# Four of eight output weights converted during attention B, two output tiles contracted in halves, denominators inverted as compact rows

## The chip, the cores and the metric

The kernel runs on one core of a Trainium2 chip. The metric is the device time of one execution in microseconds (us); the figure that is compared is the median over timed executions. TensorE multiplies matrices (PE in the profile, PEld its weight loads), VectorE (DVE), ScalarE (ACT) and GpSimd (POOL) work on tiles, SyncE (SP) issues most of the DMAs. Each engine runs its own instruction list in order, and waits on semaphores where it needs another engine or a DMA.

## The reference, cut to what matters

Two layers of a decoder run on 1024 prompt tokens and 32 sample tokens (T = 1056), model width 1024. Layer 0 is a mixture of attention A (sliding window, with sinks) and attention B (three dilated groups whose outputs are merged by their softmax denominators), times a SiLU gate, followed by one output projection, residual and layer norm:

```
mix = concat([oa, ob], -1)                 # 512 + 512 columns
mix = mix * silu(z)
y   = mix @ w_out                          # 1024 x 1024
x1  = layer_norm(alpha * x + y)
```

Layer 1 is an mLSTM in chunks of 128 tokens with its own projections, output projection and layer norm. Besides y, the caches and the states are outputs.

## The kernel before, in words

All matrix products that need float32 accuracy are made of three products of split numbers: a high part (`hi`, ScalarE) and the rest (`lo`, usually VectorE), high times high, low times high and high times low. Tokens come in three chunks `CH` of 384, 384 and 288; a chunk holds three token tiles of 128, the last one two and the 32 samples.

Layer 0 goes in stages: projections and attention A, then the gate projections with the maxima of B, then attention B proper (`attn_b`, from about 485 to 642 us), then the output projection (`out0`, `out_proj`, from 642 us). `attn_b(kv)` takes the groups 3, 2, 1 in turn. For each block of 128 queries `scores` makes scores `sc` on PE, their exponentials twice on ScalarE (`ph` rounded, `p` exact), the difference `pl` = p - ph (line 477 on GpSimd for every fourth block, `POOL_LO`; line 114 on VectorE for the others), and three products into `av`: values by ph (lines 481, 482) and by pl (line 483). `emit` adds `av` into `OD`, [65, 4, 1024], whose last row is the denominators. Beside it runs `samples()`, the attention of the sample tokens, in scratch tiles `scr` with its keys and values loaded as `KT`.

`merge0(ty, kv, c, M)` makes two of the eight feature blocks of one chunk of `mix`: it loads `mo` (numerators) and `mf` (denominators, each row broadcast to 64 partitions), multiplies, multiplies by the gate `mz`, and splits into `mh` and `ml`. For kv = 0, `finish` has already inverted the denominators as a [32, 128] tile `dn` (line 511) and written them to `FD`. For kv = 1 (`inverse=False`), `mf` is loaded from the raw denominators in `OD` and inverted after the broadcast, on VectorE, 128 partitions by 384 columns, twice per chunk (line 839).

`out_proj` contracts `mix` with the eight weight blocks k = 0 to 7 of `w_out`. A weight block is loaded as `wr` (two buffers), and split into `oh` (ScalarE) and `ol` (VectorE). Blocks 0 and 1 are made during attention B; blocks 2 to 7 go into pool `wo`, which takes memory that attention B used. One token tile takes two PSUM tiles `py` (halves of the 1024 columns) with 24 products each, in k order: line 163 (mh by oh), 164 (ml by oh), 165 (mh by ol). Line 880 then adds the residual, and `layer_norm` and the transposes `trx` follow.

The order on each engine is not that of the source: the tile framework schedules the program by its own estimates of time, with priorities set by `ahead`, and `weave` mixes the streams by the weights W1 to W4. So a change in one place can move others.

Of the kernel before, what the change touches and what calls it, by code (L numbers as in the profile page):

```python
# [4 lines left out]
F32 = mybir.dt.float32  # L5
# [61 lines left out]
POOL_LO = 4  # L67

# [5 lines left out]
class Scratch:  # L74


    def __init__(self, *tiles):
        self.free = [[t, 0] for t in tiles]
        self.tags = {}

# [15 lines left out]
class Builder:  # L96
# [57 lines left out]
    def proj_tok(self, ps, i, X, xs, w):  # L154
# [3 lines left out]
        for k in range(8):  # L158
# [289 lines left out]
    def scores(self, g, kv, hf, Q1, Q2, K1, K2, V, emit):  # L448
        nc = self.nc
        for qb in range(2 * hf, 2 * hf + 2):  # L450
# [4 lines left out]
            for bi, (kb, kind) in enumerate(bl):  # L455
# [45 lines left out]
    def finish(self, ty, kv, sink_nm=None):  # L501
# [10 lines left out]
        self.store('m', self.FD[ty][kv].rearrange("h (b q) -> (h b) q", q=128), dn)  # L512

# [48 lines left out]
    def attn_b(self, kv, done=None):  # L562
# [253 lines left out]
    def merge0(self, ty, kv, c, M, inverse=True):  # L816
# [10 lines left out]
        OD = self.OD[ty][kv]  # L827
        D = self.FD[ty][kv] if inverse else OD[64]
        for u in range(2 * ty):
            pr = slice(64 * u, 64 * u + 64)  # L830
            self.load(o[pr, :, :m], OD[0:64].rearrange("d (c u) t -> d c u t", u=2)[:, :, u, t0:t0 + m])
            self.load(F[pr, :, :m], D.rearrange("(c u) t -> c u t", u=2)[:, u, t0:t0 + m].partition_broadcast(64))
# [29 lines left out]
    def out_proj(self, M, W, xres, g, b, consume, early={}):  # L862
        nc = self.nc
        with self.tc.tile_pool(name="lnp", bufs=3) as lp:
            for i in ORDER:
                m = 128 if i < 8 else 32
                if i == 6:
                    xs = self.pair(lp, M[2])
                xr = None
                if i in early:  # L870
                    r = early[i]
                else:
                    xr = lp.tile([128, 1024], F32, tag="xr", name="xr")
                    r = [xr[:, 0:512], xr[:, 512:1024]]
                    self.load(xr[:m], xres[128 * i:128 * i + m])
                for n in range(2):
                    ps = self.pp.tile([128, 512], F32, tag=("pj", "sc")[n], name="py")
                    ns = slice(512 * n, 512 * n + 512)
                    self.proj_tok(ps, i, M, xs if i == 8 else None, lambda k: [w[:, ns] for w in W[k]])
                    nc.vector.scalar_tensor_tensor(r[n][:m], r[n][:m], ALPHA, ps[:m], op0=OP.mult, op1=OP.add)  # L880
                    for c in (32,) if i == 8 else ():
                        nc.vector.tensor_tensor(r[n][:32], ps[c:c + 32], r[n][:32], OP.add)
                self.layer_norm(m, r, g, b)
                consume(i, m, r, xr)

    def layer0(self):
# [13 lines left out]
        self.FD = [[dt(f"FD{t}{i}", [4, TP]) for i in range(2)] for t in range(2)]  # L900
        self.SZ = dt("SZ", [8, 128, T])
# [9 lines left out]
        with tc.tile_pool(name="qp", bufs=2) as self.qp, tc.tile_pool(name="kp", bufs=2) as self.kp, \  # L911
# [81 lines left out]
            def samples():  # L993
                sp = Scratch(*(self.x2p.tile([128, 3072], F32, tag=f"x{u}x2", name=f"scr{u}") for u in "hl"))
# [643 lines left out]
```

## Time and profile before

| what | value |
|---|---|
| time, median of 3 runs | 1497.02 us (1495.68 to 1500.87) |
| the profiled execution: time, span | 1504.22 us, 1501.9 us |
| granted TensorE clock, mean | 0.979 of full |
| PE busy | 1416.9 us, 94% of the span |
| DVE, ACT, POOL busy | 896.6, 514.3, 203.1 us |

The span runs from the first to the last instruction; the rest of an execution's time lies around it. The page has the busy time of each engine in 40 slices; of PE's 40 digits the lowest, a 7, is the slice from 638 to 676 us, in which attention B ends and the output projection begins. Queries on the trace give the waits, the instructions in order of time, and the chain that ended last.

### The profile page before, as it was taken

The page shows a single profiled execution, that of the slowest core. Times are in us where ns is not written, and L with a number is a line of the kernel's source. Part 1 is how long each engine was busy: PE and PEld are TensorE (multiplying, and loading weights), DVE is VectorE, ACT ScalarE, POOL GpSimd, SP SyncE. Part 2 cuts the span into 40 slices and gives each one's busy share as a digit, 9 for nine tenths or more (in the row PEclk, how much of TensorE's full clock was granted, in tenths as well). Part 3 has the DMA queues.
Part 4 walks back from the last instruction along what each step waited for, and adds up shares of the span by engine and source line. Part 5 has one row for each costly group of instructions (what it writes and reads, how often), then busy time and mean ns, then how long its engine had stood idle before and what let it go on. Part 6 is the DMA issues. An engine that isn't in the chain of part 4 may idle for free.

```text
span 1501.9 us, 22033 instructions
## 1 busy us (share of the span) xinstructions
PE 1416.9 (94%) x7862; PEld 1203.8 (80%) x7862; DVE 896.6 (60%) x2480; ACT 514.3 (34%) x939; POOL 203.1 (14%) x249
## 2 busy tenths in 40 slices
PE   8999999998899898879999999999999999998997
PEld 8989999898898544457788878988898899877785
DVE  5312457577576756669774535655565566566786
ACT  5332254542123756721133313331333133333310
POOL 1002243422321212101000000100000000000010
PEclk9999999999999989989999999999999999999999
DMA  8446565556753789564222655364323322341741
GB/s 297 168 143 196 176 194 163 173 160 178 198 172 98 234 254 246 171 200 122 96 79 76 216 198 204 105 194 131 77 78 117 117 49 69 117 129 23 241 138 46
DMA packets 139306, 226.85 MB, mean 151 GB/s; under 512 B 17216, under 2 KB 107296, under 8 KB 138680
## 3 DMA queue, kind: packets, MB, share of 16 engines
q1 hardware_dynamic: 129496, 201.96, 44.0%
q10 hardware_dynamic: 9702, 23.50, 4.5%
q8 instruction: 62, 1.02, 0.3%
q14 instruction: 46, 0.38, 0.1%
HBM read 166.60 MB, written 81.88 MB: 165 GB/s over the span
## 4 chain that ended last, share of the span: by engine, by line
PE 69%; DMA 16%; DVE 8%; issue 4%; ACT 2%; SPq 1%; POOL 0%; DVEq 0%; ACTq 0%; POOLq 0%
PE pj L197 10%; PE pj L199 10%; PE pj L198 10%; PE py L163 3%; PE py L165 3%; PE py L164 3%; PE pvo L163 3%; PE pvo L164 3%; PE pvo L165 3%; DMA G<-GR 2%; DMA OD<-OD 1%; DMA K<-KK 1%; PE st L431 1%; DMA wr<-in_wo_dram 1%; DMA out_cmems_dram<-Cs 1%
## 5 line engine op out<-in xcount | busy, mean ns | idle before, releaser
L197 PE MATMUL pj<-xh,wh 128*128 128x384 f32 (+1 forms) x576 | 189.1, 328 | 8.4 <-DVE sz L609 3.3
L197 PE MATMUL pj<-x1h,wh 128*128 128x384 f32 (+1 forms) x576 | 189.3, 329 | 1.7 <-ACT QT L1171 1.6
L199 PE MATMUL pj<-xh,wl 128*128 128x384 f32 (+1 forms) x576 | 188.4, 327 | 0.0
L198 PE MATMUL pj<-xl,wh 128*128 128x384 f32 (+1 forms) x576 | 188.3, 327 | 0.0
L199 PE MATMUL pj<-x1h,wl 128*128 128x384 f32 (+1 forms) x576 | 187.6, 326 | 0.0
L198 PE MATMUL pj<-x1l,wh 128*128 128x384 f32 (+1 forms) x576 | 187.3, 325 | 0.0
L197 PEld LDWEIGHTS pj<-xh,wh 128*128 128x128 f32 x576 | 110.4, 192 | 12.6 <-DVE sz L609 4.3
L197 PEld LDWEIGHTS pj<-x1h,wh 128*128 128x128 f32 x576 | 108.3, 188 | 6.5 <-issue 3.3
L199 PEld LDWEIGHTS pj<-x1h,wl 128*128 128x128 f32 x576 | 108.3, 188 | 6.0 <-issue 5.8
L198 PEld LDWEIGHTS pj<-x1l,wh 128*128 128x128 f32 x576 | 108.4, 188 | 4.0 <-issue 3.8
L198 PEld LDWEIGHTS pj<-xl,wh 128*128 128x128 f32 x576 | 110.3, 191 | 1.6
L199 PEld LDWEIGHTS pj<-xh,wl 128*128 128x128 f32 x576 | 110.3, 192 | 0.9
L435 DVE CUSTOM_DVE_ANT_0 junk<-st,maskr 128x256 f32<-128x256 f32 (+1 forms) x256 | 93.0, 363 | 26.7 <-PE st L431 9.5
L163 PE MATMUL pvo<-voh,x1h 128*128 128x512 f32 x256 | 102.3, 402 | 3.0 <-DVE SZ L1187 3.0
L164 PE MATMUL pvo<-voh,x1l 128*128 128x512 f32 x256 | 101.4, 399 | 0.0
L165 PE MATMUL pvo<-vol,x1h 128*128 128x512 f32 x256 | 100.6, 396 | 0.0
L808 POOL TENSOR_TENSOR rsw<-rsw,mhalf 128x1 f32<-128x1 f32 (+1 forms) x54 | 40.1, 743 | 318.7 <-DVE rsw L807 303.5
L114 DVE TENSOR_TENSOR pl<-p,ph 128x512 fp32r<-128x512 f32 x82 | 63.6, 782 | 29.0 <-ACT p L469 16.6
L110 ACT ACTIVATE wh<-wr 128x1024 fp32r<-128x1024 f32 x48 | 50.7, 1057 | 75.9 <-PE pj L198 69.9
L120 POOL TENSOR_TENSOR wl<-wr,wh 128x1024 fp32r<-128x1024 f32 x24 | 58.0, 2415 | 131.1 <-ACT qs L231 70.6
L431 PE MATMUL st<-K,QZ 128*128 128x256 f32 x256 | 52.1, 292 | 10.7 <-DMA QZ<-QQ 5.6
L163 PEld LDWEIGHTS pvo<-voh,x1h 128*128 128x128 f32 x256 | 48.8, 191 | 13.8 <-DVE SZ L1187 3.3
(352 smaller groups left out, 3165.1 us busy)
## 6 DMA issues: line engine op xcount, KB each, us to landing
Q<-QQ SPq DMA_DIRECT2D x32, 512.0 KB
out_kvs_dram<-in_cache_b_kv_dram SPq DMA_DIRECT2D x16, 1022.0 KB
wr<-in_w0f_dram SPq DMA_DIRECT2D x24, 512.0 KB
wr<-in_w1f_dram SPq DMA_DIRECT2D x24, 512.0 KB
QQ<-sh ACTq DMA_DIRECT2D x16, 512.0 KB
QQ<-sl ACTq DMA_DIRECT2D x16, 512.0 KB
QZ<-QQ SPq DMA_DIRECT2D x32, 256.0 KB
wr<-in_wo_dram SPq DMA_DIRECT2D x16, 512.0 KB
```

Of the source, the lines that this page charges most:

```text
L110: return self.nc.scalar.activation(out, in_, AF.Copy, scale=scale)
L114: return self.nc.vector.tensor_tensor(out, in_, f(hi), OP.subtract)
L120: self.nc.gpsimd.tensor_tensor(out, in_, f(hi), OP.subtract)
L163: nc.tensor.matmul(ps, xh[:, k, t], wh, start=k == 0, stop=False)
L164: nc.tensor.matmul(ps, xl[:, k, t], wh, start=False, stop=False)
L165: nc.tensor.matmul(ps, xh[:, k, t], wl, start=False, stop=k == 7)
L197: nc.tensor.matmul(ps[:, :n], wh[:, k, :], xh[:, k, :n], start=k == 0, stop=False)
L198: nc.tensor.matmul(ps[:, :n], wh[:, k, :], xl[:, k, :n], start=False, stop=False)
L199: nc.tensor.matmul(ps[:, :n], wl[:, k, :], xh[:, k, :n], start=False, stop=k == 7)
L431: nc.tensor.matmul(st[:, u, :], Q1[:, h, q0:q0 + 128], K1[:, w0:w0 + 256], start=True, stop=True)
L435: nc.vector.tensor_tensor_reduce(junk[:, :n], st[:, u, c0:c0 + n], mk, 1.0, -3e38, OP.add, OP.max, ST[:, 8 * h + qb:8 * h + qb + 1])
L808: nc.gpsimd.tensor_tensor(r, v, self.mhalf[:m], OP.pow)
```

## The change

- `samples()` now converts four weight blocks of the output projection (0 to 3) instead of two. Blocks 2 and 3 (`ox`) go into tiles `xb` and `xc` of pool `x2p`, in which the samples' scratch lay; the scratch is now three tiles of 2112 numbers instead of two of 3072. The first token chunk of layer 1's input moves to a new pool `x1p`, and layer 1's QT and KT move into `x2p`.
- `out_proj` takes the first two token tiles together: k = 0 to 3 for both, then k = 4 to 7 for both.
- kv = 1's numerators and denominators go to one DRAM tensor per chunk, `ODC[c]`. `finish_chunk(c)` loads the denominators as a [12, 128] tile `dnc` (8 rows for the last chunk), inverts it and writes `FDC[c]`; `merge0` then loads `mf` from there, and multiplies on GpSimd as it does for kv = 0.
- All `pl` are made on VectorE.

```diff
-                if g and self.nsc % POOL_LO == 0:
-                    nc.gpsimd.tensor_tensor(pl, p, f(ph), OP.subtract)
-                else:
-                    self.lo(pl, p, ph)
+                self.lo(pl, p, ph)
...
+    def finish_chunk(self, c):
+
+        n = 4 * (min(CH[c][1], TP - CH[c][0]) // 128)
+        dn = self.mp.tile([128, 2, 384], F32, tag="mf", name="dnc")[:, 0, 0:128]
+        self.store('m', dn[:n], self.ODC[c][64].rearrange("h (b q) -> (h b) q", q=128))
+        self.nc.vector.reciprocal(dn[:n], dn[:n])
+        self.store('m', self.FDC[c].rearrange("h (b q) -> (h b) q", q=128), dn[:n])
...
-                    self.store('b', self.OD[1][kv][:, :, t], OD[:, :, t])
+                    self.store('b', self.ODC[qb // 3] if kv else self.OD[1][kv][:, :, t], OD[:, :, t])
...
-            if inverse:
-                nc.gpsimd.tensor_tensor(o[:, :, :m], o[:, :, :m], F[:, :, :m], OP.mult)
-            else:
-                for a in range(2):
-                    nc.vector.reciprocal(F[:, a, :m], F[:, a, :m])
-                nc.vector.tensor_tensor(o[:, :, :m], o[:, :, :m], F[:, :, :m], OP.mult)
+            nc.gpsimd.tensor_tensor(o[:, :, :m], o[:, :, :m], F[:, :, :m], OP.mult)
...
-            for i in ORDER:
+            for grp in (ORDER[:2],) + tuple((i,) for i in ORDER[2:]):
+
+                parts = (range(4), range(4, 8)) if len(grp) > 1 else (range(8),)
...
+                for ks in parts:
+                    for i, m, r, xr, ps in todo:
+                        for n in range(2):
+                            ns = slice(512 * n, 512 * n + 512)
+                            self.proj_tok(ps[n], i, M, xs if i == 8 else None, lambda k: [w[:, ns] for w in W[k]], ks)
...
             def last(c):
+                self.finish_chunk(c)
                 if c < 2:
-                    self.merge0(1, 1, c, self.M, False)
+                    self.merge0(1, 1, c, self.M)
...
-                sp = Scratch(*(self.x2p.tile([128, 3072], F32, tag=f"x{u}x2", name=f"scr{u}") for u in "hl"))
+                sp = Scratch(*(self.x2p.tile([128, 2 * T], F32, tag=f"x{u}", name=f"scr{u}") for u in "abc"))
                 yield from self.sample_attn(sp)
-                for k in range(2):
-                    w = [self.wsp.tile([128, 1024], F32R, tag=f"w{u}", name=f"o{u}") for u in "hl"]
+                assert sp.home(self.OS) == 0
+                for k in range(4):
+                    if k < 2:
+                        w = [self.wsp.tile([128, 1024], F32R, tag=f"w{u}", name=f"o{u}") for u in "hl"]
+                    else:
+                        x = self.x2p.tile([128, 2, 1024], F32R, tag=f"x{'bc'[k - 2]}", name="ox")
+                        w = [x[:, 0, :], x[:, 1, :]]
...
-            W = self.W0 + [self.load_wo(A['wo0'], k, *self.wo_tiles(wp, k)) for k in range(2, 8)]
+            W = self.W0 + [self.load_wo(A['wo0'], k, *self.wo_tiles(wp, k)) for k in range(4, 8)]
```

The orders of all five engines are alike up to the end of the gate projections, and again from the start of layer 1 (the lines of the changed file lie 2 to 24 further on). Between them, three places.

PE, at the first products of the output projection, before: `py` are the products of token tile 0, `av` the last products of attention B.

```order
L163 MATMUL py<-oh,mh_4900 128x512
L164 MATMUL py<-oh,ml_4901 128x512
L165 MATMUL py<-ol,mh_4900 128x512
L483 MATMUL av<-pl,V 66x512
L481 MATMUL av<-ph,V 66x512
L482 MATMUL av<-ph,V 64x512
```

The same place in the changed kernel: `ox` is weight block 2 or 3.

```order
L165 MATMUL py<-oh,mh_4906 128x512
L166 MATMUL py<-oh,ml_4907 128x512
L167 MATMUL py<-ol,mh_4906 128x512
L165 MATMUL py<-ox,mh_4906 128x512
L166 MATMUL py<-ox,ml_4907 128x512
L167 MATMUL py<-ox,mh_4906 128x512
```

Where PE turned back to attention B after six products of blocks 0 and 1, it now has the products of blocks 2 and 3 ahead of it: 19 before the next `av`, 48 before it needs block 4.

DVE, at the first inversion for kv = 1, before: `mf` is the broadcast denominators of chunk 0.

```order
L839 RECIPROCAL mf<-mf 128x384 x2
L114 TENSOR_TENSOR pl<-p,ph 128x512 x2
L576 TENSOR_TENSOR OD<-av,OD 65x4x128
L114 TENSOR_TENSOR pl<-p,ph 128x512
L840 TENSOR_TENSOR mo<-mo,mf 128x768
L576 TENSOR_TENSOR OD<-av,OD 65x4x128
L841 TENSOR_TENSOR mz<-mz,mo 128x768
L576 TENSOR_TENSOR OD<-av,OD 65x4x128
L115 SCALAR_TENSOR_TENSOR ml_4901<-mz,mh_4900 128x768
L114 TENSOR_TENSOR ol<-wr,oh 128x1024 x2
```

The same place in the changed kernel, `dnc` being the compact denominators:

```order
L518 RECIPROCAL dnc<-dnc 12x128
L116 TENSOR_TENSOR pl<-p,ph 128x512 x3
L583 TENSOR_TENSOR OD<-av,OD 65x4x128
L116 TENSOR_TENSOR pl<-p,ph 128x512
L583 TENSOR_TENSOR OD<-av,OD 65x4x128
L116 TENSOR_TENSOR pl<-p,ph 128x512
L845 TENSOR_TENSOR mz<-mz,mo 128x768
L518 RECIPROCAL dnc<-dnc 12x128
L117 SCALAR_TENSOR_TENSOR ml_4907<-mz,mh_4906 128x768
L583 TENSOR_TENSOR OD<-av,OD 65x4x128
L847 TENSOR_TENSOR mz<-mz,scra 128x2x32
L116 TENSOR_TENSOR ol<-wr,oh 128x1024 x2
```

The inversion stands at the same place in the row of `pl`, on 12 partitions by 128 columns once instead of 128 by 384 twice; the second one (chunk 1) now stands ahead of the two weight splits `ol`, which are those of blocks 4 and 5 instead of 2 and 3.

SP, behind the last loads of queries, before:

```order
L104 DMA mo<-OD_92 64x2x384
L104 DMA mf<-OD_92 64x2x384
L104 DMA mo<-OD_92 64x2x384
L104 DMA mf<-OD_92 64x2x384 x2
L104 DMA mo<-OD_92 64x2x384 x2
L104 DMA mf<-OD_92 64x2x384
L104 DMA lng_6590<-in_ln_dram 128x512
L104 DMA mz<-SZ 128x2x288
L104 DMA lng_6591<-in_ln_dram 128x512
L104 DMA wr<-in_wo_dram 128x1024
```

The same place in the changed kernel, behind two loads of queries that now stand behind three of `wr`:

```order
L109 DMA dnc<-ODC_97 12x128
L106 DMA mo<-ODC_97 64x2x384 x2
L109 DMA FDC_100<-dnc 12x128
L106 DMA mf<-FDC_100 64x2x384 x2
L109 DMA dnc<-ODC_98 12x128
L106 DMA mo<-ODC_98 64x2x384 x2
L109 DMA FDC_101<-dnc 12x128
L106 DMA mz<-SZ 128x2x288
L106 DMA mf<-FDC_101 64x2x384 x2
L106 DMA wr<-in_wo_dram 128x1024
```

Each chunk has two more DMAs in a row, and the `wr` at the end, block 4 before, is block 6 now. `dnc` and `mf` share one buffer, so chunk 1's `dnc` is loaded after GpSimd has read chunk 0's `mf`.

## Rows read from the trace of the kernel before

**Rows 1.** Busy us of the engines by stretch, then clock, DMA share, GB/s.

```profile
core 0: us, PE busy (x) PEld busy (x) DVE busy (x) ACT busy (x) POOL busy (x), PEclk, DMA share, GB/s
485.00:545.00 60.00, 52.68 (x238) 31.47 (x237) 39.80 (x74) 39.61 (x71) 12.23 (x12) 0.86 0.77 231
545.00:600.00 55.00, 50.88 (x288) 27.58 (x285) 36.57 (x72) 35.38 (x68) 11.74 (x10) 0.94 0.89 255
600.00:642.00 42.00, 34.80 (x164) 20.88 (x163) 26.38 (x35) 31.15 (x55) 8.56 (x6) 1.00 0.58 175
642.00:684.00 42.00, 29.74 (x105) 21.65 (x104) 32.45 (x31) 10.39 (x12) 2.48 (x1) 0.88 0.63 190
684.00:776.00 92.00, 91.07 (x446) 73.25 (x447) 72.16 (x161) 13.90 (x26) 9.63 (x11) 1.00 0.31 103
```

**Rows 2.** Waits of PE, 480 to 700: waited for, us, times, longest.

```profile
PE av L483 <- DVE pl L114: 8.3, 4, 4.9
PE py L163 <- ACT oh L110: 4.2, 2, 3.1
...
PE av L483 <- POOL pl L477: 2.3, 3, 1.7
```

**Rows 3.** PE in order of time: start, us, [idle before].

```profile
648.56 0.69 PE L483 MATMUL av<-pl,V 128*66 128x512 f32 x1 [4.92 <-DVE pl L114]
...
667.15 0.50 PE L163 MATMUL py<-oh,mh 128*128 128x512 f32 x1 [3.13 <-ACT oh L110]
...
684.68 0.50 PE L163 MATMUL py<-oh,mh 128*128 128x512 f32 x1 [0.78 <-DVE xr L880]
```

**Rows 4.** DVE in order of time, the first inversion.

```profile
643.00 4.96 DVE L839 RECIPROCAL mf<-mf 128x384 f32<-128x384 f32 x2 [4.76 <-DMA mf<-OD]
```

**Rows 5.** DVE by line, 485 to 690: count, busy, mean ns, idle before.

```profile
L839 DVE RECIPROCAL mf<-mf 128x384 f32<-128x384 f32 (+1 forms) x6 | 13.3, 2257 | 8.6 <-DMA mf<-OD 8.6
```

**Rows 6.** Chain that ended last, 628 to 700: start, us, what.

```profile
631.60 4.29 DMA OD<-OD
...
637.90 5.01 DMA mf<-OD
...
654.02 2.79 DMA mf<-OD
...
660.82 7.17 DMA wr<-in_wo_dram
...
670.36 0.88 DVE mz L841
671.26 0.85 ACT mh L110
...
679.84 1.21 DVE ol L114
...
685.18 0.23 PE py L164
```

**Rows 7.** SP's issues around kv = 0's inversion, in order of time.

```profile
573.58 0.34 SPq L107 DMA_DIRECT2D dn<-OD  x1
...
576.35 0.33 SPq L107 DMA_DIRECT2D FD<-dn  x1
...
580.97 1.31 SPq L104 DMA_DIRECT2D mf<-FD  x2
```

**Rows 8.** Tile dn: ns min/median/max, first and last start.

```profile
L511 DVE RECIPROCAL dn<-dn x3: 914/941/941, 268.2 to 575.4; 32x128 f32<-32x128 f32 x3
```

**Rows 9.** By line: POOL, 480 to 700.

```profile
L836 POOL TENSOR_TENSOR mo<-mo,mf 128x768 f32<-128x768 f32 (+1 forms) x3 | 5.2, 1741 | 51.7 <-DMA mz<-SZ 38.1 <-DMA mf<-FD 13.6
```

**Rows 10.** By line: ACT, 485 to 690.

```profile
L110 ACT ACTIVATE oh<-wr 128x1024 fp32r<-128x1024 f32 x8 | 8.4, 1056 | 17.0 <-DMA wr<-in_wo_dram 12.9 <-PE av L483 2.2 <-PE so L728 1.9
```

**Rows 11.** Tile pl: ns min/median/max, first and last start.

```profile
L114 DVE TENSOR_TENSOR pl<-p,ph x82: 616/686/2027, 205.6 to 649.6; 128x512 fp32r<-128x512 f32 x82
L477 POOL TENSOR_TENSOR pl<-p,ph x18: 1263/1290/2481, 476.1 to 649.8; 128x512 fp32r<-128x512 f32 x18
```

**Rows 12.** Chain, 560 to 610: a load of the samples' values.

```profile
597.80 8.24 DMA KT<-in_vc_dram
```

More of the change, by code (lines that the diff above doesn't have):

```diff
@@ L65 @@
 W1, W2, W3, W4 = (129, 76), (86, 8), (77, 20, 8), (64, 90)
-POOL_LO = 4
 ORDER = (0, 1, 2, 3, 4, 5, 6, 8, 7)
@@ L79, in __init__, with home @@
         self.tags = {}
+    def home(self, x):
+        return [t.tensor for t, _ in self.free].index(x.tensor)
     def tile(self, shape, dt, tag=None, name=None):
@@ L152, in pair, with proj_tok @@
         return xs
-    def proj_tok(self, ps, i, X, xs, w):
+    def proj_tok(self, ps, i, X, xs, w, ks=range(8)):
         nc = self.nc
-        for k in range(8):
+        for k in ks:
             wh, wl = w(k)
@@ L814, in rstd, with merge0 @@
         yield w[:, 1:2]
-    def merge0(self, ty, kv, c, M, inverse=True):
+    def merge0(self, ty, kv, c, M):
         nc = self.nc
@@ L864, in out_proj @@
         with self.tc.tile_pool(name="lnp", bufs=3) as lp:
-            for i in ORDER:
[L866 to L884, printed above, removed]
+            for grp in (ORDER[:2],) + tuple((i,) for i in ORDER[2:]):
+                parts = (range(4), range(4, 8)) if len(grp) > 1 else (range(8),)
+                todo = []
+                for i in grp:
+                    m = 128 if i < 8 else 32
+                    if i == 6:
+                        xs = self.pair(lp, M[2])
+                    xr = None
+                    if i in early:
+                        r = early[i]
+                    else:
+                        xr = lp.tile([128, 1024], F32, tag="xr", name="xr")
+                        r = [xr[:, 0:512], xr[:, 512:1024]]
+                        self.load(xr[:m], xres[128 * i:128 * i + m])
+                    todo.append((i, m, r, xr, [self.pp.tile([128, 512], F32, tag=("pj", "sc")[n], name="py")
+                                               for n in range(2)]))
+                for ks in parts:
[3 more added lines that the diff above has]
+                            self.proj_tok(ps[n], i, M, xs if i == 8 else None, lambda k: [w[:, ns] for w in W[k]], ks)
+                            if ks[-1] < 7:
+                                continue
+                            nc.vector.scalar_tensor_tensor(r[n][:m], r[n][:m], ALPHA, ps[n][:m], op0=OP.mult, op1=OP.add)
+                            for c in (32,) if i == 8 else ():
+                                nc.vector.tensor_tensor(r[n][:32], ps[n][c:c + 32], r[n][:32], OP.add)
+                        if ks[-1] == 7:
+                            self.layer_norm(m, r, g, b)
+                            consume(i, m, r, xr)
@@ L900, in layer0 @@
         self.FD = [[dt(f"FD{t}{i}", [4, TP]) for i in range(2)] for t in range(2)]
+        self.ODC = [dt(f"ODC{c}", [65, 4, min(n, TP - t0)]) for c, (t0, n) in enumerate(CH)]
+        self.FDC = [dt(f"FDC{c}", [4, min(n, TP - t0)]) for c, (t0, n) in enumerate(CH)]
         self.SZ = dt("SZ", [8, 128, T])
@@ L1004, in layer0 @@
                   (ahead(tc, merges((0, 1)), AHEAD[1]), W3[2]))
-            self.merge0(1, 1, 2, M, False)
+            self.merge0(1, 1, 2, M)
             run(merges((2,)))
@@ L1017, in out0 @@
                 self.load_ln(0, gb)
-                tags = (("x2", self.x2p), ("0", self.xp), ("1", self.xp))
+                tags = (("x1", self.x1p), ("0", self.xp), ("1", self.xp))
                 self.XT1 = []
@@ L1165, in proj_head @@
         else:
-            QT = self.hp.tile([128, 2, T], F32, tag="QT", name="QT", bufs=1)
-        KT = self.hp.tile([128, 2, T], F32, tag="KTh", name="KTh")
+            QT = self.x2p.tile([128, 2, T], F32, tag="xa", name="QT")
+        KT = self.x2p.tile([128, 2, T], F32, tag="xbxc"[2 * (h % 2):][:2], name="KTh")
         self.heads[h] = [QT, KT]
@@ L1422, in layer1 @@
                                                              for u in "hl")))
-                    for k, t in ((2, "KTh"), (3, "QT")):
-                        x = self.hp.tile([128, 2, 1024], F32R, tag=t, name=f"o{k}", bufs=2 if k == 2 else 1)
+                    for k, t in ((2, "xb"), (3, "xa")):
+                        x = self.x2p.tile([128, 2, 1024], F32R, tag=t, name=f"o{k}")
                         W.append(self.load_wo(A['wo1'], k, x[:, 0, :], x[:, 1, :]))
@@ L1499, in body @@
             self.x2p.release()
+            self.x1p.release()
 def arrays(inp):
```

13 lines of the change are left out of this document (8 added, 5 removed).

## The prediction

> **What bounds the kernel now.** I read the busy times by stretch first, then the waits of PE in the stretches that are not full, then PE, VectorE and the chain in order of time. The stretches [rows 1] show that PE is the bound almost everywhere: from 684 to 776 us it is busy for 91.1 of 92 us. It is not full in attention B (485 to 642: 138.4 of 157 us) and in the start of the output projection (642 to 684: 29.7 of 42 us, at a mean granted clock of 0.88, so part of that ran at 1.2 instead of 2.4 GHz). The change works in these two stretches alone; the order of the rest is as it was, and a PE that is full there hands on every microsecond won or lost before.
>
> In 642 to 684 us PE has 105 products [rows 1]. At the full clock one starts each 0.23 us [rows 6], so the work is 24 us, and 18 of the 42 us are loss: idle time and the low clock behind it. Two things make it. First, VectorE stands before its first inversion: it waits 4.76 us for `mf`, then inverts for 4.96 us, with `pl` queued behind [rows 4], and PE is idle for 4.92 us for that `pl` [rows 3]. Second, PE has only blocks 0 and 1 to multiply with; block 2 can be written only when attention B's memory is free, and 4 and 5 are loaded after it. PE waits 4.2 us for `oh` [rows 2], 3.13 of them at 667 us [rows 3], and does not start the third token tile before 684.68 us [rows 3]. In attention B itself the waits are many and short; 2.3 us of them are for a `pl` made on GpSimd [rows 2].
>
> **The inversions.** Removed are six inversions with 13.3 us of VectorE and 8.6 us of idle time before them [rows 5]. Added are three of a tile like `dn`; the nearest row is 0.94 us on 32 partitions [rows 8], which I take for 12 and 8 as well. Price of the new path: after the store of the numerators two more DMAs stand in the chain. For kv = 0 the same pair is in the trace: `dn` is issued at 573.58 [rows 7] and the inversion starts at 575.4 [rows 8], 1.8 us; `FD` is issued at 576.35 and the load behind it at 580.97 [rows 7], 4.6 us. I take these as they are; the bounds for each of the two are 1.8 and 4.6 us. The multiply goes to GpSimd: 1.83 us, 5.2 us for three of which one is the shorter form [rows 9].
>
> The Trainium skill (DMA: Bandwidth & Descriptors, Anatomy of one DMA) gives any DMA a fixed cost of about 2.0 us whatever its size, which speaks against trading VectorE time for two small transfers. By it the two hops would be 4.0 us instead of my 6.4, and the sum below some 4 us better, because two chunks pass through them one after the other.
>
> **Where the chain then ends.** I start at the store of chunk 0, 631.60 us, and leave attention B as it was. The store lands after 4.29 us [rows 6], at 635.9; `dnc` is there at 637.7; inverted at 638.7, when VectorE had nothing else to do before (it was idle from 638.2 to 643.0 [rows 4]), so `pl` follows at once and the stall of 4.92 us goes. `FDC` has landed at 643.3, two loads are issued, `mf` is there after 5.01 us [rows 6] at 648.9 (low end 2.79 us [rows 6]). GpSimd multiplies until 650.7, `mz` 0.88 and `mh` 0.85 us [rows 6] end at 652.5; ScalarE then makes `oh` of blocks 4 and 5, 1.06 us each [rows 10], at 653.5 and 654.6. PE meanwhile has 48 products of blocks 0 to 3 and some ten `av`, 13 us, from about 642 to 655, and then 24 of blocks 4 and 5, to about 661. So the first of PE's waits for `oh` goes too: its work is what blocks 2 and 3 give it.
>
> What is late next is blocks 6 and 7. On SP their loads stand behind `mf` of chunk 1, whose `dnc` waits for GpSimd to have read chunk 0's `mf` (650.7). The chain again: `dnc` 652.5, inverted 653.5, `FDC` landed 658.1, two issues, `wr` of block 6 issued at about 659.5; it takes 7.17 us [rows 6], 666.7. Block 7 follows some 1.7 us later, 668.4. Its `ol` is behind the third inversion, for which the chain gives: `mf` of chunk 1 at 664, multiplied at 666, `dnc` at 668, inverted at 669, `ol` 1.21 us [rows 6] at about 671. Four products and the residual later, at 673.3, the third tile starts, against 684.68: 11.4 us won.
>
> Bounds of this term. With both hops at 1.8 us and `mf` at 2.79, block 7 is there at 662 and PE only ends its work at about 667: 17 us won, near the 18 that are there at all. With both hops at 4.6 us block 7's `ol` comes at 678.5 and the tile at 680: 4.6 us won.
>
> **The low parts.** GpSimd's `pl` takes 1.29 us, VectorE's 0.69 [rows 11]. The 18 moved ones put 12.4 us on VectorE, and the inversions take 10.5 off, so its load stays at about two thirds of attention B [rows 1]. I take the 2.3 us that PE waited for GpSimd [rows 2] as won. Bounds: VectorE's own `pl` is waited for as well (8.3 us, of which 4.92 is the inversion [rows 2, 3]), so the gain can be nothing, or a loss of 12.4 us if every moved `pl` were waited for in full.
>
> The Trainium skill (SBUF — State Buffer, SBUF: two separate sides) says that GpSimd and VectorE share a port pair which one operation locks for its whole length. By it the three multiplies that move to GpSimd could hold VectorE for up to 1.83 us each. I count nothing for it, since VectorE is idle around them; by the rule the sum would be at most 2 us worse, as only chunk 0's falls among `pl`.
>
> **The other edits.** Blocks 2 and 3 are now split in attention B: 2.1 us of ScalarE and 2.4 of VectorE [rows 6, 10] beside a PE that is busy 83 to 92% there; they leave the stretch in which ScalarE and VectorE are waited for. Their cost is nothing as long as they are not ahead of a `ph` or `pl` that PE needs; else up to 4.5 us. The halves of the first two tiles cost no product, and layer 1's tiles only change their place. Attention B's instructions are shuffled by the scheduler: PE's idle time there is 18.6 us [rows 1], and that this part comes out 5 us better or worse I take as open, with zero as the value.
>
> **Sum.** 11.4 + 2.3 = 13.7 us off the profiled execution of 1504.2 us (its span of 1501.9 and 2.3 around it): 1490.5. That execution was 7.2 us above the median of the runs; the same 13.7 us off the median of 1497.0 give 1483.
>
> **Rivals.** (1) The hops are dear: the chain of DMAs through one buffer, twice in a row, decides when block 7 comes. With 4.6 us for each hop the gain is 4.6 us, at most 7 with the low parts: 1490 to 1492. For it speaks the 4.6 us of `FD`; against it that the DMA share falls to 0.58 behind 600 us [rows 1], and `FD`'s hop lay where it was 0.89.
>
> (2) All is hidden: hops of 1.8 us, the fuller PE keeps its clock, and attention B wins by its shorter `pl`. 17 + 2.3, and up to 3 more: 1475 to 1478. Against it stands the long way to block 7.
>
> (3) Attention B gives back what the projection wins: the gain of 11 to 14 us meets a loss of the same size in the shuffled stretch, and the time is 1493 to 1501.
>
> (4) Slower: SP's queue. The loads of the samples' values (`KT`) and of the last queries stand in one row with loads that must wait for a buffer. The last two pairs of queries now stand behind `wr` of blocks 4 and 5, which need the buffers of blocks 2 and 3, which need the end of the samples' attention, which needs `KT`. One `KT` took 8.24 us [rows 12]. If two are late in full, PE, which takes its list in order, stands for 16.5 us, and the time is 1500; with three, 1508. It decides from 14 us of such waiting on. Against it: PE has about 20 us of attention B left behind the samples' end in the new order, and the queries need some 15.
>
> **How the numbers follow.** The forecast (1478 to 1488 us) has 0.50, (1) 0.17, (2) 0.13, (3) 0.12, (4) 0.08. About 0.3%, 4.5 us, is what a measurement can tell from no change: faster is below 1492.5. The forecast, (1) and (2) make 0.80 for faster, (3) is 0.12 for the same, (4) 0.08 for slower. The range 1474 to 1494 holds the first three and leaves out most of the others.
>
> **What would show it.** Right: no wait of PE for `pl` of 4 us behind 640; 48 products of blocks 0 to 3 before a wait for `oh`; the one wait left there for blocks 6 and 7; the third tile 10 to 15 us earlier, and layer 1 shifted by as much. The hops show as the issues of `dnc`, `FDC` and `mf` on SP. Wrong: PE's first output product later than 642 us by more than 3, waits of PE for `KT` or queries, or a block 7 that comes later than 675.

## The result, and the profile after

Six executions of each kernel: 1489.51 us median (1485.73 to 1491.71) after the change, 1498.0 us before, ratio 0.9944 with an interval of 0.9923 to 0.9964: 8.4 us faster. The forecast was 1483 us and 14 us of gain. The time alone lies between the forecast's 1478 to 1488 us and rival (1)'s 1490 to 1492; only the trace tells the two apart. The profiled execution after took 1490.2 us (span 1488.4).

The stretches of [rows 1], in the kernel after the change (columns as there):

```profile
485.00:545.00 60.00, 49.50 (x233) 29.41 (x234) 43.43 (x82) 39.52 (x72) 4.04 (x6) 0.91 0.78 227
545.00:600.00 55.00, 45.11 (x206) 23.97 (x205) 34.94 (x71) 32.72 (x64) 5.73 (x6) 0.91 0.83 240
600.00:642.00 42.00, 38.79 (x228) 23.06 (x227) 32.32 (x46) 33.33 (x57) 0.04 (x1) 1.00 0.61 189
642.00:684.00 42.00, 36.03 (x146) 27.84 (x147) 23.29 (x38) 9.52 (x13) 5.76 (x5) 0.96 0.57 186
684.00:776.00 92.00, 90.15 (x456) 73.34 (x456) 69.49 (x152) 18.33 (x33) 8.75 (x10) 1.00 0.31 106
```

In 642 to 684 us PE now has 146 products instead of 105 and a granted clock of 0.96 instead of 0.88. In 485 to 600 us it does less than before: 94.6 us busy instead of 103.6.

The waits of PE from 480 to 700 us, as in [rows 2] (waited for, us, times, longest):

```profile
PE av L480 <- ACT ph L470: 8.7, 6, 2.7
PE av L482 <- DVE pl L116: 3.2, 7, 0.7
...
PE sc L464 <- ACT p L471: 2.9, 2, 2.5
PE py L165 <- ACT oh L112: 2.9, 1, 2.9
PE av L480 <- DMA Q<-QQ: 2.8, 1, 2.8
```

The longest wait for a low part is 0.7 us instead of 4.92: the stall behind the first inversion is gone. The waits that grew stand in attention B, for ScalarE's exponentials and for a load of queries. PE in order of time, answering to [rows 3]:

```profile
644.80 0.40 PE L165 MATMUL py<-oh,mh 128*128 128x512 f32 x1
...
655.74 0.50 PE L165 MATMUL py<-oh,mh 128*128 128x512 f32 x1 [1.58 <-DVE OD L583]
...
667.08 0.50 PE L165 MATMUL py<-oh,mh 128*128 128x512 f32 x1 [2.88 <-ACT oh L112]
...
675.75 0.51 PE L165 MATMUL py<-oh,mh 128*128 128x512 f32 x1 [1.28 <-DVE xr L893]
```

The first output product comes at 644.80 instead of 642.06, the one wait for weights (2.88 us, blocks 6 and 7) ends at 667.08, and the third token tile starts at 675.75 instead of 684.68, 8.9 us earlier (the forecast's sign was 10 to 15). That is close to the 8.4 us of the medians, in one execution of each kernel. The spans of the two profiled executions are further apart, 13.5 us; the rest lies behind this point, in work that is the same in both. Here is the stretch from the third tile to the end, before and then after:

```profile
684.68:1501.90 817.22, 790.01 (x4396) 672.12 (x4396) 497.77 (x1528) 225.58 (x463) 48.42 (x128) 0.99 0.38 119
```

```profile
675.75:1488.40 812.65, 788.59 (x4396) 671.71 (x4396) 497.94 (x1530) 226.23 (x464) 49.68 (x129) 1.00 0.38 121
```

It is the same 4396 products, and 4.6 us lie between two executions of them (granted clock 0.99 and 1.00). The first 800 of them take 149.4 us in both, so the 4.6 us arise later, in layer 1, whose order the change leaves as it was. Two more executions of the changed kernel's instructions (e2 and e12 below) have 810.9 and 810.4 us, and the profiled execution before was 6.2 us above the median of 1498.0. Whether the change has any part in this is not shown.

The chain that ended last, after the change, from the store of chunk 0's numerators on, against [rows 6] (start, us, what):

```profile
634.81 4.17 DMA ODC<-OD
639.04 1.42 DMA dnc<-ODC
...
641.51 2.03 DMA FDC<-dnc
...
644.24 4.94 DMA mf<-FDC
649.39 1.85 POOL mo L844
...
654.31 2.33 DMA FDC<-dnc
...
657.29 4.58 DMA mf<-FDC
...
667.15 6.11 DMA mz<-SZ
```

Each hop of the new path stands here once for chunk 0 and, from 654 us on, again for chunk 1.

**Two lengths tell where the time went.** B's first product with V (475.0 us before, 472.3 after) is a mark that all kernels of this study share. From it to the first output product is attention B; from there to the third token tile is the projection's start. Together the two hold the same products in every kernel. The border moves a little: in the kernel before, e5 and e9 four more products of attention B (0.9 us at 0.23) stand in the start than in the others (in e3 one). The expectations below also speak of PE's loss in the start: its length less 23 to 24 us, the work of its products at 0.23 us. "Idle in B" is attention B's length less PE's busy time in it.

| kernel | attention B | start | sum | idle in B | ratio of times |
|---|---|---|---|---|---|
| before | 167.0 | 42.6 | 209.6 | 18.6 | 1 |
| after | 172.5 | 31.0 | 203.4 | 24.4 | 0.9944 |
| after, same rows (e2) | 176.6 | 28.3 | 204.9 | 25.6 | 0.9961 |
| after, again (e12) | 172.8 | 29.0 | 201.8 | 25.3 | 0.9939 |
| before + compact inversions (e8) | 165.3 | 40.1 | 205.3 | 22.3 | 1.0000 |
| before + low parts on VectorE (e5) | 165.8 | 49.8 | 215.6 | 21.3 | 1.0046 |
| early weights alone (e9) | 171.1 | 43.0 | 214.0 | 19.1 | 0.9999 |
| after, low parts back (e1) | 170.9 | 29.1 | 200.0 | 19.7 | 0.9923 |
| the same, again (e11) | 173.1 | 30.2 | 203.3 | 20.0 | 0.9936 |
| after, own buffer (e3) | 175.4 | 31.8 | 207.2 | 24.7 | 0.9959 |
| after, small multiplies on GpSimd (e4) | 172.2 | 31.2 | 203.4 | 20.2 | 0.9962 |
| after, reciprocals' loads on GpSimd (e6) | 174.6 | 30.6 | 205.2 | 22.5 | 0.9945 |
| after, merge loads on GpSimd (e7) | 177.1 | 27.4 | 204.5 | 28.4 | 0.9963 |
| low parts back + merge loads on GpSimd (e10) | 167.6 | 29.6 | 197.1 | 21.0 | 0.9915 |

Three executions of one row of instructions (after, e2, e12) differ by 4.1 us in attention B, 2.7 in the start, 3.1 in the sum and 1.2 in the idle time, so a single profile's length is read to about 4 us. The intervals of the ratios are 0.2 to 0.3% to either side.

The two stretches as the traces show them, attention B and then the start, in the kernel before and then in the changed one (columns as in [rows 1]):

```profile
475.04:642.06 167.02, 148.38 (x740) 89.24 (x738) 108.46 (x185) 110.61 (x201) 33.82 (x29) 0.93 0.74 220
642.06:684.68 42.62, 29.68 (x105) 21.59 (x104) 33.13 (x32) 10.39 (x12) 2.48 (x1) 0.88 0.62 190
```

```profile
472.33:644.80 172.47, 148.12 (x744) 89.07 (x742) 120.48 (x209) 112.88 (x204) 9.81 (x12) 0.94 0.74 217
644.80:675.75 30.95, 25.21 (x102) 19.35 (x100) 13.88 (x18) 7.36 (x9) 3.69 (x2) 0.94 0.64 210
```

Of the 11.7 us that the start became shorter, 7.2 are idle time of PE and 4.5 busy time: fewer products stand in it, and the granted clock is 0.94 instead of 0.88.

### The profile page after: what moved, and what is told of

It reads as the page before. It is cut to its first block, busy times and chain, and to the rows that moved or that the text cites. A ratio compares the mean times of both kernels' runs of the same rounds, so it can differ in the third digit from the quotient of the medians.

```text
span 1488.4 us, 22044 instructions
## 1 busy us (share of the span) xinstructions
PE 1408.9 (95%) x7862; PEld 1198.7 (81%) x7862; DVE 888.6 (60%) x2492; ACT 513.6 (35%) x939; POOL 181.4 (12%) x234
## 4 chain that ended last, share of the span: by engine, by line
PE 70%; DMA 17%; DVE 7%; issue 3%; ACT 2%; SPq 1%; POOL 1%; DVEq 0%; POOLq 0%; ACTq 0%
PE pj L199 11%; PE pj L200 10%; PE pj L201 10%; PE py L165 3%; PE py L167 3%; PE py L166 3%; PE pvo L165 3%; PE pvo L166 3%; PE pvo L167 3%; DMA G<-GR 2%; DMA Q<-QQ 2%; PE st L433 1%; DMA K<-KK 1%; DMA QZ<-QQ 1%; DMA out_cmems_dram<-Cs 1%
## 5 line engine op out<-in xcount | busy, mean ns | idle before, releaser
L116 DVE TENSOR_TENSOR pl<-p,ph 128x512 fp32r<-128x512 f32 x100 | 74.3, 753 | 30.7 <-ACT p L471 17.6
L815 POOL TENSOR_TENSOR rsw<-rsw,mhalf 128x1 f32<-128x1 f32 (+1 forms) x54 | 40.1, 743 | 310.3 <-DVE rsw L814 294.3
```

What stands on the lines that cost most here:

```text
L116: return self.nc.vector.tensor_tensor(out, in_, f(hi), OP.subtract)
L815: nc.gpsimd.tensor_tensor(r, v, self.mhalf[:m], OP.pow)
```

## The experiments

**e5: the low parts alone.** Every `pl` of the kernel before on VectorE:

```
-POOL_LO = 4
+POOL_LO = 10**6
```

> The kernel before with all low parts of attention B on VectorE, nothing else of the change; its order is kept but for that, so that the cost of this one edit is seen apart from the new order. Before, attention B lasts 167.0 us from its first product with V to the first output product, and the third token tile starts 209.6 us after that first product. Theory A (the low parts slow attention B on VectorE): B lasts 170 to 172.5, and the time is 1500 to 1503 us. Theory B (they cost little; the new order of the loads makes B longer): B lasts 166 to 168.5 and the time is 1496 to 1499. Forecast: 2.3 us faster, 1496.

Measured: 1505.01 us, ratio 1.0046 (1.003 to 1.0063): 7 us slower, more than either theory gave. Attention B lasts 165.8 us, not longer than before. The loss is in the start, 49.8 instead of 42.6 us. VectorE there in order of time, in this run:

```profile
652.68 4.96 DVE L839 RECIPROCAL mf<-mf 128x384 f32<-128x384 f32 x2 [1.79 <-DMA mf<-OD]
657.57 2.29 DVE L114 TENSOR_TENSOR ol<-wr,oh 128x1024 fp32r<-128x1024 f32 x2
```

and PE:

```profile
658.78 0.80 PE L165 MATMUL py<-ol,mh 128*128 128x512 f32 x1 [5.24 <-DVE ol L114]
```

The second inversion now stands ahead of the low parts of blocks 2 and 3; in the kernel before it stood behind them. The scheduler, given other places for `pl`, put VectorE's row in another order there too. So theory B holds for attention B, and the price came through a row that the edit doesn't name.

**e8: the inversions alone.** The kernel before with `finish_chunk`, the chunks' own tensors and the multiply on GpSimd:

```
...
+                self.finish_chunk(c)
                 if c < 2:
-                    self.merge0(1, 1, c, self.M, False)
+                    self.merge0(1, 1, c, self.M)
...
```

> The kernel before with only the inversions in compact rows (the chunks' numerators and denominators in tensors of their own, the multiply on GpSimd); low parts and weights as before, so only blocks 0 and 1 are loaded early. Forecast's theory (the early blocks cover the chain): PE's wait of 4.92 us for the low part goes, but PE then waits for block 2 as before; the third token tile starts 3 to 6 us earlier than 209.6 us after B's first product with V, and the time is 1492 to 1495 us. Rival (the inversions alone are the gain, the early blocks are not needed): the tile starts 8 us earlier or more and the time is 1488 to 1491. Rival (the serial chain of small loads is worse without the early blocks): no gain, 1496 to 1499.

Measured: 1498.64 us, ratio 1.0000 (0.9983 to 1.0017): no gain; the third tile is 4.3 us earlier in the profile, the start 2.5 us shorter. PE's waits in it, 630 to 700 us:

```profile
PE py L163 <- ACT oh L110: 4.9, 2, 3.7
PE py L163 <- DVE OD L584: 3.6, 1, 3.6
PE py L163 <- DVE xr L885: 2.4, 1, 2.4
```

The wait for `pl` is gone, as forecast, and others take its place: two for blocks (4.9 us), one at the end of B (3.6), one for a residual (2.4). The third tile comes earlier as the forecast's theory had it; the time is that of the second rival, no gain.

**e9: the early weights alone.** The changed kernel with the low parts back and the old inversions:

```
...
-                self.finish_chunk(c)
                 if c < 2:
-                    self.merge0(1, 1, c, self.M)
+                    self.merge0(1, 1, c, self.M, False)
...
```

> Of the change only the four early weight blocks (with their place in memory): low parts as before, the inversions as before (whole rows on VectorE, broadcast first). It leaves out the compact inversions, which alone gave no gain. Theory C (the early blocks alone are the gain): PE's loss between its first output product and the third token tile, 18.7 us before and 6.1 in the run with the low parts back, falls to 6 to 9, and the time is 1487 to 1489 us. Forecast's theory (both edits are needed: with the old inversions PE waits for a low part behind the first inversion, 4.9 us, and blocks 4 to 7 come late, behind the other inversions): the loss stays at 12 to 17 us and the time is 1492 to 1496.

Measured: 1499.82 us, ratio 0.9999 (0.9971 to 1.0028); the start takes 43.0 us, a loss of 19.1. PE's waits in it, 630 to 700 us:

```profile
PE py L165 <- ACT oh L112: 4.8, 1, 4.8
PE av L485 <- DVE pl L116: 3.9, 1, 3.9
PE py L167 <- DVE ol L116: 3.8, 1, 3.8
```

Blocks 2 and 3 are there, but PE stands for a low part behind the first inversion (3.9), for one behind the second (3.8), and for a late block (4.8). With e8 this is the clearest finding: neither edit alone gains anything, both together (e1) gain 0.77%. A stall that one of them removes is covered by the next one unless the other edit is there too. Theory C falls; the loss is also above the 12 to 17 us of the forecast's theory, and the time above its 1492 to 1496.

**e1 and e11: low parts back on GpSimd.**

```
+                if g and self.nsc % 4 == 0:
+                    nc.gpsimd.tensor_tensor(pl, p, f(ph), OP.subtract)
+                else:
+                    self.lo(pl, p, ph)
-                self.lo(pl, p, ph)
```

> The changed kernel with every fourth low part of attention B back on GpSimd, all else kept (the scheduler orders the work anew). In the changed kernel's trace attention B, from its first product with V to the first output product, lasts 172.5 us against 167.0 before. Theory A (VectorE, now with all low parts, holds attention B up): B shrinks by 3 to 5.5 us and the time falls to 1484 to 1487 us. Theory B (the length of B comes from the new order and from the loads that stand in SyncE's row, not from the low parts): B stays within 2 us of 172.5, the waits of 2.3 us for GpSimd's low parts come back, and the time is 1489 to 1492 us. In the forecast the low parts were a gain of 2.3 us: 1492.

Measured: 1487.09 us, ratio 0.9923 (0.9901 to 0.9945). B is 170.9 us, within 2 of 172.5 as theory B has it, and PE waits 3.1 us for GpSimd's low parts again; but the time is at the edge of theory A's 1484 to 1487.

> The changed kernel with every fourth low part of attention B back on GpSimd, a second time, on the same chip as the changed kernel itself (next run). If the low parts on VectorE cost time in the changed kernel's order, it is 2 to 5 us faster than the next run again (first time: 0.9923 of the time before against 0.9944); if that was chance, the two agree within 1.5 us.

Measured: 1486.78 us, 0.9936 (0.9909 to 0.9962), beside 1488.42 for the changed kernel itself: 1.6 us apart. The mean of the two ratios with the low parts back is 0.993, that of the three without (after, e2, e12) 0.9948: 2.8 us, with intervals that overlap. What is shown is that the move to VectorE brought nothing; that it costs some 3 us is likely, not shown.

**e12: the changed kernel again,** no edit.

> The changed kernel itself, a second time, beside the run before it. Low parts cost time: 1489 to 1492 us and 2 to 5 us above that run. No cost: within 1.5 us of it. Its profile shows how far attention B's length (172.5 us from the first product with V to the first output product) and the third token tile's start (203.4 us) vary from one execution to the next; by another kernel with the same row of instructions, 176.6 and 204.9.

Measured: 1488.42 us, 0.9939 (0.9918 to 0.996). The lengths are in the table.

**e2: blocks 2 and 3 written at the projection's start.**

```
-                for k in range(4):
+                for k in range(2):
...
-            W = self.W0 + [... self.wo_tiles(wp, k)) for k in range(4, 8)]
+            W = self.W0 + [... self.ox(k) if k < 4 else self.wo_tiles(wp, k) ... for k in range(2, 8)]
```

> The changed kernel with only output weight blocks 0 and 1 loaded and split within the samples' generator; blocks 2 and 3 keep their place in memory but their loads are written at the start of the output projection. Forecast's theory (blocks 2 and 3 ready early are what covers the chain to block 7): if the scheduler puts the two loads late, PE has only 24 products of blocks 0 and 1 before it waits, the third token tile starts 4 to 8 us later, and the time is 1493 to 1497 us. Rival (the two splits, 2.1 us of ScalarE and 2.4 of VectorE inside attention B, are what lengthened it): B shrinks by 3 to 5 us and the time stays at 1488 to 1490. If the loads stay early because the memory is free early, nothing changes: 1489 to 1490.

Measured: 1491.0 us, 0.9961 (0.9936 to 0.9986). The scheduler puts out the same rows on all five engines as for the changed kernel: the loads go where their memory is free, wherever they are written. So this run is the changed kernel once more. The same is true of the two halves of the first two tiles: written without them, with `range(8)` for all tiles, the rows are the same on every engine. That part of the change does nothing; what lets 48 products of blocks 0 to 3 come first is the memory of blocks 2 and 3.

**e3: a buffer of its own for the denominators.**

```
-        dn = self.mp.tile([128, 2, 384], F32, tag="mf", name="dnc")[:, 0, 0:128]
+        dn = self.mp.tile([128, 32], F32, tag="dnc", name="dnc")
```

> The changed kernel with a buffer of its own for the compact denominators (48 rows of 32 instead of 12 rows of 128, so that it fits), not the buffer of the broadcast reciprocals; chunk 1's denominators need no longer wait until GpSimd has read chunk 0's reciprocals. Theory A (the serial chain through one buffer sets when the last blocks come, as forecast): chunk 1's chain ends 3 to 4 us earlier (its multiply on GpSimd at 658.5 to 659.5 us against 662.4 when attention B ends alike), the third token tile starts 2 to 4 us earlier, and the time is 1486 to 1487.5 us. Theory B (the loads of blocks 6 and 7 wait for the staging buffers that VectorE's low parts of blocks 4 and 5 set free, which stand behind a multiply of chunk 2 that waits for its own load): the chain is shorter and the tile no earlier by more than 1 us: 1488.5 to 1490.

Measured: 1491.1 us, 0.9959 (0.9937 to 0.998), no better than after. GpSimd's multiply of chunk 1 comes 16.1 us behind the first output product instead of 17.6: 1.5 us earlier, not 3 to 4, as the second inversion then stands behind chunk 0's `mz` on VectorE. And this, on VectorE, and SyncE's issue for block 7 behind it, took the gain back:

```profile
667.04 0.42 DVE L847 TENSOR_TENSOR mz<-mz,scra 128x64 f32<-128x64 f32 x1 [6.57 <-DMA mz<-SZ]
667.38 1.21 DVE L116 TENSOR_TENSOR ol<-wr,oh 128x1024 fp32r<-128x1024 f32 x1
```

```profile
668.62 0.33 SPq L106 DMA_DIRECT2D wr<-in_wo_dram  x1
```

A multiply of 0.42 us waits 6.57 us for gates of chunk 2, which nothing needs yet; the low part of block 5 stands behind it, and the load of block 7 waits for the staging buffer that it reads; PE itself stood 3.98 us for that low part. Theory B's mechanism is seen, in one execution: the 1.5 us are less than the start varies by (2.7).

**e4: those small multiplies on GpSimd.**

```
-            nc.vector.tensor_tensor(z[:, :, m:n], z[:, :, m:n], self.OS[:, j:j + 2, :], OP.mult)
+            nc.gpsimd.tensor_tensor(z[:, :, m:n], z[:, :, m:n], self.OS[:, j:j + 2, :], OP.mult)
```

> The changed kernel with chunk 2's small multiplies for the samples' columns (128x64) on GpSimd instead of VectorE, where each waits for a load of gates with the low parts of blocks 4 and 5, and later the residual of the first tile, behind it. Theory B (VectorE's row, held by a load, sets the loads of blocks 6 and 7 and the end of the first tiles): block 6's load is issued 1 us earlier or more, the residual 1.5 us earlier, and the third tile starts 1.5 to 3 us earlier: 1486.5 to 1488 us. Theory A (only the chain of denominators counts): the tile starts within 0.5 us of the same place: 1489 to 1490.

Measured: 1492.66 us, 0.9962 (0.9941 to 0.9983); the third tile is where it was, 203.4 us behind B's first product. Block 6's load is issued 1 us earlier, as theory B had it, and ScalarE shows why that is worth nothing. SyncE's issue for block 6 first, then ScalarE in order of time, in this run:

```profile
658.44 0.54 SPq L106 DMA_DIRECT2D wr<-in_wo_dram  x1
```

```profile
666.10 0.84 ACT L112 ACTIVATE mh<-mz 128x768 fp32r<-128x768 f32 x1 [11.08 <-DVE mz L845]
666.85 1.99 ACT L112 ACTIVATE oh<-wr 128x1024 fp32r<-128x1024 f32 x2
```

The halves of blocks 6 and 7 stand behind chunk 1's `mh` on ScalarE, and that waits for chunk 1's chain. So theory A gives the place and theory B what comes next: with the row freed the chain decides (e4), with the chain shortened the row does (e3).

**e6 and e7: merge loads off SyncE.** e6 moves the loads of `mf` for kv = 0 to GpSimd's queue, e7 all loads of `mo` and `mf`:

```
-            self.load(F[pr, :, :m], F1...)
+            (self.load if kv else nc.gpsimd.dma_start)(F[pr, :, :m], F1...)
```

What they test in the changed kernel is this piece of its chain in attention B, 560 to 600 us:

```profile
576.15 0.64 SPq L106
...
578.21 6.81 DMA Q<-QQ
...
586.27 6.59 DMA Q<-QQ
...
592.87 0.41 PE av L480
```

SyncE issues the reciprocals' loads, and behind them the queries that PE then waits for.

> The changed kernel with the broadcast reciprocals of kv = 0 (FD to mf) loaded by GpSimd's queue instead of SyncE's, so that the K, the queries and the samples' values behind them on SyncE no longer wait until GpSimd has read the buffer. Theory B (SyncE's row holds attention B up): PE's waits of 2.77 and 1.79 us near 593 and 597 us go or halve, the samples' products end 4 to 10 us earlier (141.8 us after B's first product with V now, 131.0 before), B lasts 168 to 170.5 instead of 172.5, and the time is 1485 to 1487.5 us. Rival (ScalarE's and VectorE's rows hold it, whatever queue loads): B stays at 171.5 or more and the time at 1489 to 1490.5.

Measured: 1491.26 us, 0.9945 (0.9927 to 0.9963). The two waits are gone and the samples end 140.3 us behind B's first product instead of 141.8; a wait of 2.4 us for the samples' values came instead, and B is 174.6 us. PE's idle time in B is 22.5 us, 2 to 3 less than in the three executions of the changed kernel, but B is no shorter. As far as one execution tells, the rival holds: that queue is not what lengthens attention B.

> As the run before, and in addition the numerators (mo) and the reciprocals of kv = 1 are loaded by GpSimd's queue, so that in the output projection's start the loads of blocks 6 and 7 no longer stand behind chunk 1's reciprocals on SyncE. Theory B: B as in the run before; block 6's load is issued when VectorE has set its staging buffer free, 1 us earlier, and the third token tile starts up to 1 us earlier than there: 1484 to 1487 us. Rival (chunk 1's chain itself, through ScalarE's row, in which the halves of blocks 6 and 7 stand behind chunk 1's gate product, sets the end): no gain over the run before beyond 0.5 us; and if the queue of GpSimd is slower by 1 us for each load, 2 us worse than there.

Measured: 1494.97 us, 0.9963 (0.9942 to 0.9983). The start is the shortest of all, 27.4 us (a loss of 4.4), B the longest, 177.1. The earlier tile of theory B came, its time did not; the intervals of e6 and e7 overlap, so whether GpSimd's queue costs time is not shown.

**e10: low parts back and merge loads on GpSimd** (both edits above).

> The changed kernel with every fourth low part back on GpSimd, and the numerators and reciprocals of the merges loaded by GpSimd's queue instead of SyncE's. Theory (the two gains add up): PE's loss after the first output product falls from 6.1 us (low parts back) to 4.5, as it fell from 8.0 to 4.4 with GpSimd's loads alone, attention B as with the low parts back (170.9 us to the first output product): 1484 to 1487 us. Rival (GpSimd, which again makes low parts that PE waits for, now has them behind its own loads, which wait for stores): attention B is 2 to 5 us longer than with the low parts back, and the time is 1488 to 1492.

Measured: 1485.25 us, 0.9915 (0.989 to 0.9941), the lowest time of all. The start is 29.6 us (a loss of 6.6, not 4.5); what is better is attention B, 167.6 us, for which no theory asked. PE's idle time in B, 21.0 us, is about that of e1 and e11 (19.7 and 20.0); the difference is busy time, 146.5 us against 151.2 and 153.1, at granted clocks of 0.95 against 0.94 and 0.92. It is ahead of the changed kernel by 3 us in the same set of runs, with intervals that overlap.

## Why the prediction was right, and where its sum was not

**The inversions and the chain: right.** From the first output product to the third tile the forecast had 642.06 to 673.3, 31.2 us; three executions show 31.0, 28.3 and 29.0, against 42.6 before. The stall of 4.92 us went, 48 products of blocks 0 to 3 came before a wait for weights, and that wait was for blocks 6 and 7. One of the forecast's signs of being wrong stands at its limit: the first output product, at 644.80 us, is 2.7 us later than 642, and in e2 and e12 it comes at 650.39 and 647.22, more than the 3 us allowed.

Hop by hop: the store came 3.2 us later (634.81 for 631.60); the `dnc` hop took 1.5 us (forecast 1.8), the `FDC` hop 2.1 (4.6), `mf` 4.9 (5.0), GpSimd 1.85 (1.83). The dear hop of [rows 7] was dear where it stood: the DMA share was 0.90 through its 4.62 us. The same store in the changed kernel, at 574.73 us, let the load behind it go after 1.42 us, at a share of 0.05. Rival (1) rested on the dear hop and falls. The Trainium skill (DMA: Bandwidth & Descriptors, Anatomy of one DMA) names about 2.0 us whatever the size, for the path through GpSimd; the trace has 2.03 and 2.33 for `FDC` and 1.42 and 1.54 for `dnc`, all issued by SyncE, so the stores come near that figure and the loads stay below it.

One number was right for a wrong reason. Block 6's load was forecast at 659.5, behind `mf` of chunk 1 on SyncE. It came at 659.41, because VectorE's low part of block 4 ended then, 2.34 us late behind a small multiply that waited for gates. The next multiply of that kind held VectorE once more just before the residual that freed the third tile's accumulator. VectorE in the changed kernel, in order of time:

```profile
658.03 0.23 DVE L847 TENSOR_TENSOR mz<-mz,scra 128x64 f32<-128x64 f32 x1 [2.34 <-DMA mz<-SZ]
658.17 2.36 DVE L116 TENSOR_TENSOR ol<-wr,oh 128x1024 fp32r<-128x1024 f32 x2
...
673.36 0.23 DVE L847 TENSOR_TENSOR mz<-mz,scra 128x64 f32<-128x64 f32 x1 [3.14 <-DMA mz<-SZ]
...
675.01 1.88 DVE L893 SCALAR_TENSOR_TENSOR xr<-xr,py 128x512 f32<-128x512 f32 x3
```

I had priced no wait of VectorE for those gates. The 31 us are therefore in part luck. Counted from the first output product, block 7's low part was ready at 25.4 us instead of the forecast's 28.9, mostly by the cheap hops; the last step, forecast at 2.3 us, took 5.5, with PE at a granted clock of 0.50 from 668.57 to 671.97 us and the residual behind the small multiply. The two errors cancel.

**The low parts: wrong in sign.** The 2.3 us were not won. In the order of before the move cost 7 us, through the second inversion's place in VectorE's row (e5); in the changed kernel taking it back costs nothing and may gain 3 us (e1, e11). The step that failed is "I take the 2.3 us that PE waited for GpSimd [rows 2] as won": where `pl` is made also decides how the scheduler sets the rows, so that PE's waits for GpSimd went, but its idle time in attention B rose from 18.6 to 24.4 us (19.7 and 20.0 with the low parts back).

**The other edits: priced at nothing; attention B became longer.** Attention B became 5.5 us longer in the profile (9.6 and 5.8 in the other two). The four executions with the early weights and GpSimd's low parts have 171.1, 170.9, 173.1 and 167.6 us, the three without the early weights 167.0, 165.3 and 165.8: 4.6 us by the means, and a further 3.8 with all low parts on VectorE (172.2 to 177.1 in seven profiles). The first figure is about the forecast's bound for the splits of blocks 2 and 3, "up to 4.5 us", but it is not what that bound priced, PE waiting behind the splits: PE's idle time in B is 20.7 us by the mean of the three and 20.0 of the four. What grew is PE's busy time, 145.3 to 150.7 us, at granted clocks of 0.93 to 0.97 and 0.92 to 0.95. One row of instructions varies by 3.6 us in it (147.45 to 151.03), so a cost of the early weights in attention B is not shown.

The further 3.8 us are idle time, which goes from 20.0 to 24.4. PE's wait for ScalarE's `ph` is 2.9 to 5.8 us in attention B of the four and 7.0 to 11.6 in the seven. At one place PE stands for it 1.9 to 2.8 us in each of the seven: on ScalarE, `ph` stands behind the split of a block of queries, which waits 3.0 to 3.9 us for its load. At another PE stands 2.5 us in each, and `ph` stands behind exponentials of the samples (`scrc`). The first of the two, on ScalarE in the changed kernel:

```profile
535.12 1.06 ACT L370 ACTIVATE Q<-Q 64x1024 fp32r<-64x1024 f32 x1 [3.78 <-DMA Q<-QQ]
```

So what attention B loses with all low parts on VectorE shows as waits for ScalarE, whose row is another one then. No run moves those two instructions alone, so this cause is seen and not tested; the waits that e6 took away stand elsewhere in attention B, and its length stayed. As attention B gave back about half of what the start won, rival (3) holds in part.

**The sum.** Forecast 11.4 + 2.3 + 0 = 13.7. By the three profiles: 42.6 less 29.4, so 13.2 won in the start; 174.0 less 167.0, so 7.0 lost in attention B (0.9 of each is the four products that changed sides); 6.2 net, against 8.4, 5.8 and 9.1 in the medians' ratios of 0.9944, 0.9961 and 0.9939. Rival (2) fell with B. Rival (4) did not come: PE's longest wait for queries was 2.8 us.

## What to carry to other kernels

Two stalls that end at nearly the same time hide each other: here each edit alone measured 0.0%, and the pair 0.8%, so such edits are judged together. Where a scheduler sets the rows, an edit is also a new order: compare the rows far from it, and look for a small instruction that waits for something not yet needed with something urgent behind it. Repeat one row of instructions before reading a single profile; here that moved a mark by 3 to 4 us.

## What the runs showed of the hardware

A GpSimd low part that takes 1.29 us took 5.31 while VectorE worked without a break. GpSimd, then VectorE, in the run with the low parts back:

```profile
614.34 5.31 POOL L479 TENSOR_TENSOR pl<-p,ph 128x512 fp32r<-128x512 f32 x1 [5.89 <-ACT p L471]
625.32 1.29 POOL L479 TENSOR_TENSOR pl<-p,ph 128x512 fp32r<-128x512 f32 x1 [5.67 <-ACT p L471]
```

```profile
614.00 1.22 DVE L116 TENSOR_TENSOR ox<-wr,ox 128x1024 fp32r<-128x1024 f32 x1
615.14 0.69 DVE L116 TENSOR_TENSOR pl<-p,ph 128x512 fp32r<-128x512 f32 x1
615.74 1.22 DVE L116 TENSOR_TENSOR ox<-wr,ox 128x1024 fp32r<-128x1024 f32 x1
616.87 1.05 DVE L586 TENSOR_TENSOR OD<-av,OD 65x512 f32<-65x512 f32 x1
617.83 0.68 DVE L116 TENSOR_TENSOR pl<-p,ph 128x512 fp32r<-128x512 f32 x1
```

VectorE is free at 618.5, and GpSimd ends 1.14 us later, about the length of its instruction alone; PE waited 2.7 us for it. In e11 (5.82 us) and e9 (4.96) it is the same. In e10 it took 3.40 us and ended 1.15 us behind two `pl`, while VectorE was at an `OD`, one input of which, `av`, lies in PSUM. The Trainium skill (SBUF — State Buffer, SBUF: two separate sides) says that the two engines share a port pair that one instruction locks for its whole length, on VectorE's side one with two inputs in SBUF, as the subtractions here have; the trace agrees, and adds that a row of VectorE instructions can hold GpSimd through all of them, in three of the four executions through an `OD` as well. The prediction had weighed this only the other way round, GpSimd holding VectorE.
